# Layer-0 attention: scaling the heads' outputs instead of their probabilities

## The chip, the cores and the metric

One program runs on one core of a Trainium2 chip. The metric is the device time of one execution, in microseconds. The kernel before was run three times (1480.88, 1485.19 and 1488.71 us), and one further execution was profiled.

## The reference, cut to what matters

A sequence of 512 tokens of width 1024 goes through three layers. Layer 0 mixes windowed attention (8 query heads of 64 columns, 2 key/value heads) with a pooling branch, layer 1 mixes dense latent attention with a recurrent block, and each is followed by an MLP. A third block holds sparse attention, dilated attention and a gate. The change concerns layer 0's attention alone. Each query block of 128 sees the keys of its own and the two neighbouring blocks, and a learned sink enters the denominator:

```python
m = jnp.maximum(jnp.max(s, axis=-1, keepdims=True), sk)
p = jnp.exp(s - m)
p = p / (jnp.sum(p, axis=-1, keepdims=True) + jnp.exp(sk - m))
out = jnp.einsum('bnhgqj,bnjhd->bnqhgd', p.astype(v.dtype), vb)
```

Here the division is by row of `p`, one number for each query and head, so it can also be made on `out`.

## The kernel before, in words

Activations lie transposed: 128 channels on the partitions, 512 tokens along the free axis. A product in float32 is made of three TensorE passes over operands split in two parts (`hi`, `lo`), so every weight unit and every activation has a split: the `hi` part by `copy` (line 581, ScalarE or GpSimd, whichever the program takes to be free first), the `lo` part by `tt` (line 591, VectorE or GpSimd) or by VectorE.

The order of the instructions on each engine is fixed when the program is written out. A planner keeps a clock of its own (`fl.now`), which each matmul moves on, and a guess of when VectorE, ScalarE and GpSimd come free, made of a cost for each operation (`cost`, line 329). Work that evacuates or splits is a task: a generator that goes on when its due time has come on the planner's clock (`chains`, line 387). The engines themselves take their instructions in the written order and wait by semaphores. So a task that is written early on a wrong guess makes the engine wait on the chip, with all that is queued behind it.

Layer 0's attention runs under `fl.run(attend(...), fill, fl.share)`. `attend` (line 1141) writes the scores of up to three heads ahead of their products, and lets the products of three heads go on side by side. Where attention can't go on, the program takes a step of `fill`: the query blocks, then the pooling branch, then the first half of the output projection (`out_proj`, line 1197), which uses only the pooling branch. The second half, which uses the heads' outputs `yhl[4]` to `yhl[7]`, is appended when attention is written out, and then the rest of `fill` is run.

A head goes so. `score` writes three score tiles, each followed by a task `expo`: VectorE takes the row maximum (`mx`) and its negative (`nm`), ScalarE the exponential (`p`) with its row sum (`den`). When the three tasks are done, `finish` (line 1049) adds the sink's term (`es`), takes the reciprocal (`w4`; the trace writes it as `w`), and `weigh` (line 1066) multiplies the four query blocks of `p` by it, each with one `copy` (`p<-p,w` in the trace). Only then does `weigh` set `self.done`, for which `apply` (line 1094) waits. `apply` transposes `p` on TensorE (`tr<-cst,p`, line 565), splits the transposes from PSUM into `ph` and `pl`, and multiplies by `v` (`av`). `combine` (line 1132) adds the two halves of the result into `ya`: ScalarE copies one half (`cmb`), VectorE adds the other. Two heads share one `ya`; after the second one `store` (line 1373) splits it into `yhl[4 + i]` (`hi<-ya`, `lo<-ya`).

PSUM's eight banks are shared by four tags; `tr`, the tag of the transposes, may hold five of them in this phase.

Of the kernel before, what the change touches and what calls it, by code (L numbers as in the profile page):

```python
# [13 lines left out]
AF = mybir.ActivationFunctionType  # L14
# [4 lines left out]
P = 128  # L19
# [3 lines left out]
NQ = T // P  # L23
# [465 lines left out]
def tile_hybrid(ctx: ExitStack, tc: tile.TileContext, wt, xT, pT, prm_d, cst_d, out):  # L489
# [6 lines left out]
    V, S, G = (_Engine(fl, e, k) for e, k in ((nc.vector, "V"), (nc.scalar, "S"), (nc.gpsimd, "G")))  # L496
# [13 lines left out]
    def uid(s):  # L510
        cnt[0] += 1
        return f"{s}{cnt[0]}"

    def blk(name="b", dt=F32, n=T):
        return bp.tile([P, TB], dt, tag="b", bufs=NB, name=uid(name))[:, 0:n]

    def small(n, name="s", dt=F32):
        return sp.tile([P, n], dt, tag=f"s{n}", bufs=24, name=uid(name))
# [6 lines left out]
    def bank(tag):  # L525
        spare = len(banks) - sum(1 for k in held if k != tag and not held[k])
        if held[tag] >= getattr(fl, tag) or spare < 1 or min(banks) > fl.now:
            return None
        banks.remove(min(banks))
        held[tag] += 1  # L530
        return pp.tile([P, T], F32, tag="ps", bufs=8, name=uid(tag))
# [6 lines left out]
    def takec(tag):  # L538
        while (t := bank(tag)) is None:
            yield 0.1  # L540
        return t

    def give(tag):
        banks.append(max(fl.now, fl.last) + 0.1)
        held[tag] -= 1
# [6 lines left out]
    def waitc(*tasks):  # L552
        for t in tasks:
            while not t.done:
                yield 0.1
# [8 lines left out]
    def tr(o, i, idn):  # L564
        PE.transpose(o, i, idn)  # L565
        fl.now += 0.11
# [37 lines left out]
    class Unit:  # L604
        def __init__(self, name, i, cuts=1):
            self.name, self.i = name, i
            t = _WT[name]
            self.n = min(1024, _WN[t][1] - 1024 * i)
            self.left = self.n
            self.raw = self.hi = self.lo = self.task = None  # L610
            self.parts = [(self.n * c // cuts, self.n * (c + 1) // cuts) for c in range(cuts)]
            self.at, self.ready = [], 0
            self.kept = None
# [162 lines left out]
    def C(name, n=None):  # L776
        o = _CO[name][0]
        n = n or _CO[name][1]
        if o + n <= NKEEP:
            return cst[:, o:o + n]  # L780
        t = blk("cst")
        nc.sync.dma_start(t[:, :n], cst_d[:, o:o + n])
        return t

    def PR(name, i=0, n=1):
        o, w = _PO[name]
        return prm[:, o + i:o + i + n]

    ident = C("ident")
# [42 lines left out]
    def split_to(act, ps, scale=None):  # L832
        act.hi, act.lo = blk("hi", F32R), blk("lo", F32R)
        yield from split_ps(ps, act.hi, act.lo, scale)
        yield
        act.done = True
# [155 lines left out]
    class Head:  # L992
# [2 lines left out]

        def __init__(self, passes, rng, masks, v, scale=1.0, nsink=None, sink=None, gate=None):
            self.passes, self.rng, self.masks, self.v = passes, rng, masks, v
            self.scale, self.nsink, self.sink, self.gate = scale, nsink, sink, gate  # L1000
            self.done = False
            self.join = None

        def expo(self, qbs, ps):
# [44 lines left out]
        def finish(self, tasks):  # L1049

            yield from waitc(*tasks)
            if self.sink is not None:
                es = small(4, "es")
                S.activation(es, self.nm, AF.Exp, bias=self.sink, scale=1.0)
                yield
                V.tensor_add(self.den, self.den, es)
            else:
                V.tensor_scalar(self.den, self.den, 1e-30, None, op0=ALU.max)
            w4 = small(4, "w4")
            V.reciprocal(w4, self.den)  # L1060
            if self.gate is not None:
                V.tensor_mul(w4, w4, self.gate)
            yield
            yield from self.weigh(w4)

        def weigh(self, w4):
            for qb in range(NQ):
# [64 lines left out]
    def combine(po, dst):  # L1132

        t = blk("cmb")
        copy(t[0:64], po[64:128])
        yield
        V.tensor_add(dst, po[0:64], t[0:64])
        give("av")
        yield
# [21 lines left out]
    SC64 = 0.125  # L1161
# [53 lines left out]
    def next_norm(gcol, *sums):  # L1215

        h = acts()

        def then(c):
            go(split_to(h[c], x[c], gcol(c)))  # L1220
            for ss, sc in sums:
                go(ss.add(x[c], None if sc is None else sc(c)))
            yield

        return h, then
# [3 lines left out]
    h = acts()  # L1229
# [26 lines left out]
    nsink = cons.tile([P, 8], F32, name="nsink")  # L1256
# [113 lines left out]
    fill = [q_blocks(), pooling(), out_proj("eout", yhl, 0)]  # L1370
    yz = {}

    def store(hd, base, post=None):

        def done(po):
            i = hd // 2
            if i not in yz:
                yz[i] = [blk("ya"), 0]
            y = yz[i][0]
            yield from combine(po, y[64 * (hd % 2):64 * (hd % 2) + 64])  # L1380
            yz[i][1] += 1
            if yz[i][1] == 2:
                del yz[i]
                if post is not None:
                    yield from post(i, y)
                yield from split_to(yhl[base + i], y)
        return done

    def job0(hd):
        st = {}  # L1390

        def score():
            g = hd // 4
            q = qs[hd]
            st["h"] = Head([(q, ks[g][0]), (q, ks[g][1])], band3, band3_masks, lambda kb: v0[0](kb, g),
                           SC64, nsink=nsink[:, hd:hd + 1], sink=PR("sink", hd))
            return st["h"].score()

        return (lambda: hd in qs and 1 in ks and v0 and nmask.done, score,
                lambda: st["h"].apply(done=store(hd, 4)))  # L1400

    fl.phase("a")
    fl.run(kv_blocks(), None)
    fl.run(attend([job0(i) for i in range(8)], fl.ahead, fl.streams), fill, fl.share)
    ss = SumSq(NC)
    h, then = next_norm(lambda c: PR("n_mlp0", c), (ss, None))
# [98 lines left out]
    h = h2  # L1505
# [255 lines left out]
    def job1(hd):  # L1761
        st = {}

        def score():
            (qh, ql), (kh, kl) = qt[hd], kt[hd]
            st["h"] = Head([(qh, kh), (ql, kh), (qh, kl)], full, {},
                           lambda kb: vt[hd // 2](kb, hd % 2))
            return st["h"].score()

        return (lambda: hd in qt and hd in kt and hd // 2 in vt, score,  # L1770
                lambda: st["h"].apply(done=store(hd, 4)))
# [10 lines left out]
    h, then = next_norm(lambda c: PR("n_mlp1", c), (ss, None))  # L1782
# [15 lines left out]
    h = h2  # L1798
# [326 lines left out]
    def nsa_jobs(hd):  # L2125
# [41 lines left out]
        def app():  # L2167
            yield from st[0].apply(last=False, before=cmp_apply)
            yield from st[1].apply(first=False, prev=st[0], done=store(hd, 2, gate_z))
# [217 lines left out]
    h = h2  # L2387
# [26 lines left out]
```

## Time and profile before

| | |
|---|---|
| three runs | 1480.88, 1485.19 (median), 1488.71 us |
| profiled execution, its own time | 1481.19 us |
| its span, first to last instruction | 1479.4 us |
| mean granted TensorE clock | 0.993 |
| TensorE busy | 1450.2 us (98%) |
| VectorE busy | 906.4 us (61%) |
| ScalarE busy | 639.5 us (43%) |
| GpSimd busy | 328.3 us (22%) |
| DMA | 291.44 MB, mean 197 GB/s |

Busy times are sums over the whole span; the share in one stage can be very different. PE is TensorE, PEld its weight loads, DVE is VectorE, ACT is ScalarE, POOL is GpSimd. Most instructions are written by a helper, so they share a line (L561 matmuls, L565 transposes, L363 all of the three other engines) and are told apart by the names of their tiles.

### The profile page before, as it was taken

Reading aid. Unit: us, or ns where it says so; the run is one execution under the profiler, and the core shown is the slowest. Engines: PE = TensorE matmul, PEld = TensorE weight load, DVE = VectorE, ACT = ScalarE, POOL = GpSimd, SP = SyncE. Lnnn points to the kernel's source line nnn. Section 1 sums busy time; section 2 is a strip of 40 time slices with the busy share of each in tenths; the row PEclk is TensorE's granted clock in tenths of the full one; section 3 lists DMA queues with packets and bytes.
Section 4 is the critical chain, followed back from the end, with each engine's and each line's share of the span. In section 5 each row is a group of like instructions: output and inputs, shape, how many; then the busy total and the mean of one; then the engine's idle time right before and its main releaser. Section 6 shows DMA issues by size and latency. Waiting matters only on the chain.

```text
span 1479.4 us, 18899 instructions
## 1 busy us (share of the span) xinstructions
PE 1450.2 (98%) x6789; PEld 1175.9 (79%) x6789; DVE 906.4 (61%) x1414; ACT 639.5 (43%) x1175; POOL 328.3 (22%) x307
## 2 busy tenths in 40 slices
PE   8999999999999999799999999999999999999998
PEld 5777878888888887688888888888887788888787
DVE  7896865646434458987675665756755566536413
ACT  5684433323223345477343433334521575324623
POOL 5441220202102026542120210202110000110332
PEclk9999999999999999899999999999999999999999
DMA  6113688898333363331599999999855323346352
GB/s 220 44 43 100 209 276 284 284 290 283 108 100 101 141 221 130 127 129 72 188 312 332 334 325 331 320 334 320 305 204 201 114 86 115 114 174 216 109 196 88
DMA packets 118317, 291.44 MB, mean 197 GB/s; under 512 B 13136, under 2 KB 14672, under 8 KB 118224
## 3 DMA queue, kind: packets, MB, share of 16 engines
q1 hardware_dynamic: 118080, 289.98, 57.7%
q8 instruction: 53, 0.87, 0.2%
q14 instruction: 40, 0.33, 0.1%
q10 hardware_dynamic: 144, 0.26, 0.1%
HBM read 205.26 MB, written 84.93 MB: 196 GB/s over the span
## 4 chain that ended last, share of the span: by engine, by line
PE 90%; DVE 5%; DMA 2%; ACT 1%; issue 1%; POOL 0%; SPq 0%; POOLq 0%; DVEq 0%; ACTq 0%
PE mm L561 78%; PE sc L561 4%; PE tr L565 3%; PE av L561 3%; DVE sg L363 2%; PE tr L561 1%; DMA kr<-in_wt_dram 1%; DVE lo L363 1%; DVE wl L363 1%; DMA pin<-in_pT_dram 0%; DMA x<-in_xT_dram 0%; ACT wh L363 0%; DMA wk<-khi 0%; ACT sg L363 0%; POOL ma L363 0%
## 5 line engine op out<-in xcount | busy, mean ns | idle before, releaser
L561 PE MATMUL mm<-hi,wh 128*128 128x512 f32 (+1 forms) x1276 | 508.4, 398 | 0.8 <-POOL wh L363 0.5
L561 PE MATMUL mm<-hi,wl 128*128 128x512 f32 (+1 forms) x1276 | 502.1, 393 | 4.8 <-DVE wl L363 2.7
L561 PE MATMUL mm<-lo,wh 128*128 128x512 f32 (+1 forms) x1276 | 500.2, 392 | 0.3 <-POOL lo L363 0.3
L561 PEld LDWEIGHTS mm<-hi,wl 128*128 128x128 f32 x1276 | 241.0, 189 | 56.1 <-DVE wl L363 4.2
L561 PEld LDWEIGHTS mm<-lo,wh 128*128 128x128 f32 x1276 | 240.9, 189 | 55.3 <-POOL lo L363 0.8
L561 PEld LDWEIGHTS mm<-hi,wh 128*128 128x128 f32 x1276 | 241.2, 189 | 53.0 <-issue 1.1
L363 ACT ACTIVATE khi<-kr 128x512 fp32r<-128x512 f32 x120 | 75.9, 632 | 304.6 <-DMA kr<-in_wt_dram 298.3
L561 PE MATMUL mm<-ul,wh 128*128 128x512 f32 x512 | 201.6, 394 | 0.3 <-DVE ul L363 0.3
L561 PE MATMUL mm<-uh,wh 128*128 128x512 f32 x512 | 201.6, 394 | 0.0
L561 PE MATMUL mm<-uh,wl 128*128 128x512 f32 x512 | 201.5, 394 | 0.0
L363 DVE TENSOR_TENSOR wl<-wr,wh 128x1024 fp32r<-128x1024 f32 (+1 forms) x145 | 182.9, 1262 | 6.2 <-ACT wh L363 5.6
L363 DVE TENSOR_TENSOR klo<-kr,khi 128x512 fp32r<-128x512 f32 x150 | 121.4, 810 | 81.8 <-ACT khi L363 73.1
L363 ACT ACTIVATE wh<-wr 128x1024 fp32r<-128x1024 f32 (+1 forms) x147 | 148.8, 1013 | 47.6 <-PE mm L561 34.4
L363 DVE TENSOR_TENSOR x<-x,mm 128x512 f32<-128x512 f32 x112 | 76.8, 686 | 147.1 <-PE mm L561 143.7
L363 POOL TENSOR_TENSOR ma<-ma 128x512 f32<-128x512 f32 x62 | 86.6, 1397 | 279.3 <-ACT uh L363 237.6
L561 PEld LDWEIGHTS mm<-ul,wh 128*128 128x128 f32 x512 | 96.1, 188 | 23.8 <-DVE ul L363 1.3
L561 PEld LDWEIGHTS mm<-uh,wl 128*128 128x128 f32 x512 | 96.2, 188 | 22.3
L561 PEld LDWEIGHTS mm<-uh,wh 128*128 128x128 f32 x512 | 96.1, 188 | 22.3
L363 ACT ACTIVATE p<-sc,nm 128x512 f32<-128x512 f32 (+3 forms) x136 | 75.3, 557 | 27.8 <-DVE nm L363 24.8
L363 POOL TENSOR_SCALAR khi<-kr 128x512 fp32r<-128x512 f32 x30 | 29.6, 986 | 248.1 <-DMA kr<-in_wt_dram 225.8
L363 DVE TENSOR_TENSOR pl<-tr,ph 128x512 fp32r<-128x512 f32 (+2 forms) x108 | 66.3, 624 | 27.9 <-ACT ph L363 27.1
L363 DVE SCALAR_TENSOR_TENSOR ma<-mm,rb 128x512 f32<-128x512 f32 x64 | 44.1, 690 | 59.0 <-PE mm L561 58.9
(293 smaller groups left out, 1633.4 us busy)
## 6 DMA issues: line engine op xcount, KB each, us to landing
wr<-in_wt_dram SPq DMA_DIRECT2D x144, 512.0 KB, 5.2
kr<-in_wt_dram SPq DMA_DIRECT2D x150, 256.0 KB, 5.8
wk<-khi SPq DMA_DIRECT2D x150, 256.0 KB, 5.9
wk<-klo SPq DMA_DIRECT2D x150, 256.0 KB, 5.7
wh<-wk SPq DMA_DIRECT2D x74, 512.0 KB, 3.3
wl<-wk SPq DMA_DIRECT2D x74, 512.0 KB, 4.2
x<-xs SPq DMA_DIRECT2D x16, 256.0 KB, 5.0
cst<-in_cst_dram SPq DMA_DIRECT2D x8, 256.0 KB, 5.1
```

The costliest lines, as they stand in the source:

```text
L363: return fn(*a, **k)
L561: PE.matmul(o, l, r, start=start, stop=stop, skip_group_check=True)
L565: PE.transpose(o, i, idn)
```

## The change: what it does

For layer 0's heads `finish` writes the reciprocals into a column range of a tile `w8` that two heads share (8 columns: 4 query blocks of 2 heads), and `weigh` isn't called. `self.done` is set as soon as the exponentials are done, ahead of the sink's term and the reciprocal. The probabilities stay unscaled through the transposes and the product with `v`. When both heads of a pair stand in `ya`, `weigh_pair` spreads the 8 columns into a block `wb` of 128x512 on ScalarE (64 columns for each query block and head), transposes it in four pieces of 128x128 on TensorE into a `tr` bank, and multiplies `ya` by that bank on VectorE. Then `ya` is split as before. The heads of the other layers keep `weigh`.

```diff
-        def __init__(self, passes, rng, masks, v, scale=1.0, nsink=None, sink=None, gate=None):
+        def __init__(self, passes, rng, masks, v, scale=1.0, nsink=None, sink=None, gate=None, w4=None):
...
-            self.done = False
+            self.w4 = w4
+            self.done = self.weighed = False
...
             yield from waitc(*tasks)
+            self.done = self.w4 is not None
...
-            w4 = small(4, "w4")
+            w4 = small(4, "w4") if self.w4 is None else self.w4
             V.reciprocal(w4, self.den)
...
             yield
-            yield from self.weigh(w4)
+            self.weighed = True
+            if self.w4 is None:
+                yield from self.weigh(w4)
...
+    def weigh_pair(heads, w8):
+
+        def post(i, y):
+            while not all(h.weighed for h in heads):
+                yield 0.1
+            t = blk("wb")
+            S.activation(t.rearrange("p (b h e) -> p b h e", b=NQ, h=2),
+                         w8.rearrange("p (h b) -> p b h", h=2).unsqueeze(3).to_broadcast([P, NQ, 2, 64]), AF.Copy)
+            yield
+            ps = yield from takec("tr")
+            for b in range(NQ):
+                tr(ps[:, b * P:(b + 1) * P], t[:, b * P:(b + 1) * P], ident)
+            yield
+            V.tensor_mul(y, y, ps)
+            give("tr")
+            yield
+        return post
...
+    pairs = [([], small(8, "w8")) for _ in range(4)]
+
     def job0(hd):
         st = {}
+        heads, w8 = pairs[hd // 2]
...
-                           SC64, nsink=nsink[:, hd:hd + 1], sink=PR("sink", hd))
+                           SC64, nsink=nsink[:, hd:hd + 1], sink=PR("sink", hd),
+                           w4=w8[:, 4 * (hd % 2):4 * (hd % 2) + 4])
+            heads.append(st["h"])
...
-                lambda: st["h"].apply(done=store(hd, 4)))
+                lambda: st["h"].apply(done=store(hd, 4, weigh_pair(heads, w8))))
```

## Rows read from the trace of the kernel before

**Rows 1.** The page, its head and busy times: engine, busy us, share, instructions.
```profile
span 1479.4 us, 18899 instructions
PE 1450.2 (98%) x6789; PEld 1175.9 (79%) x6789; DVE 906.4 (61%) x1414; ACT 639.5 (43%) x1175; POOL 328.3 (22%) x307
```
**Rows 2.** Busy time by stretch around attention: stretch, its length, busy us, clock, DMA.
```profile
46.00:84.00 38.00, 37.97 (x205) 30.87 (x204) 33.52 (x79) 29.02 (x76) 14.86 (x21) 1.00 0.13 43
84.00:113.00 29.00, 24.57 (x142) 19.50 (x141) 26.58 (x60) 25.78 (x63) 15.40 (x15) 1.00 0.17 49
113.00:124.00 11.00, 11.00 (x60) 9.37 (x59) 7.22 (x13) 5.66 (x11) 1.78 (x2) 1.00 0.32 112
124.00:164.00 40.00, 40.00 (x177) 32.45 (x175) 28.67 (x41) 18.09 (x28) 3.23 (x2) 1.00 0.37 118
```
**Rows 3.** What TensorE waited for, 40 to 125 us: total us, times, longest.
```profile
PE av L561 <- DVE pl L363: 2.3, 2, 1.9
PE mm L561 <- DVE wl L363: 1.2, 2, 0.6
PE av L561 <- ACT ph L363: 0.4, 1, 0.4
PE mm L561 <- POOL lo L363: 0.3, 1, 0.3
```
**Rows 4.** Groups by shape, 40 to 125 us: count | busy us, mean ns.
```profile
L363 ACT ACTIVATE p<-p,w 128x384 f32<-128x384 f32 x13 | 7.8, 608 | 0.0
L363 ACT ACTIVATE p<-p,w 128x256 f32<-128x256 f32 x10 | 5.0, 503 | 2.1 <-DVE w L363 2.1
L363 POOL TENSOR_SCALAR p<-p,w 128x256 f32<-128x256 f32 x6 | 2.9, 484 | 10.0 <-DVE w L363 5.8 <-PE mm L561 3.6 <-ACT ph L363 0.6
L363 POOL TENSOR_SCALAR p<-p,w 128x384 f32<-128x384 f32 x3 | 1.8, 590 | 1.3 <-ACT p L363 1.3
L363 DVE TENSOR_TENSOR rbb<-tr,cst 128x512 f32<-128x512 f32 x3 | 2.1, 685 | 0.0
L363 ACT ACTIVATE zs<-mm 128x512 f32<-128x512 f32 x2 | 1.1, 574 | 0.0
```
**Rows 5.** The chain of waits, 120 to 170 us: start, us, what.
```profile
168.12 0.44 PE tr L565 x4
```
**Rows 6.** ScalarE in order of time: head 0's copies; ahead of two weight splits.
```profile
52.24 0.56 ACT L363 ACTIVATE p<-sc,nm 128x384 f32<-128x384 f32 x1
57.20 1.02 ACT L363 ACTIVATE p<-p,w 128x256 f32<-128x256 f32 x2 [1.40 <-DVE w L363]
60.41 0.50 ACT L363 ACTIVATE p<-p,w 128x256 f32<-128x256 f32 x1
...
83.85 0.60 ACT L363 ACTIVATE p<-p,w 128x384 f32<-128x384 f32 x1
84.36 1.05 ACT L363 ACTIVATE wh<-wr 128x1024 fp32r<-128x1024 f32 x1
...
95.65 0.61 ACT L363 ACTIVATE p<-p,w 128x384 f32<-128x384 f32 x1
96.16 1.05 ACT L363 ACTIVATE wh<-wr 128x1024 fp32r<-128x1024 f32 x1
```
**Rows 7.** All engines in order of time around the longest wait.
```profile
108.17 2.37 POOL L363 TENSOR_TENSOR wl<-wr,wh 128x1024 fp32r<-128x1024 f32 x1
109.37 2.25 DVE L363 TENSOR_TENSOR wl<-wr,wh 128x1024 fp32r<-128x1024 f32 x1 [0.58 <-ACT wh L363]
111.54 0.55 DVE L363 TENSOR_TENSOR pl<-tr,ph 128x384 fp32r<-128x384 f32 x1
112.14 0.45 PE L561 MATMUL av<-pl,v 128*128 128x384 f32 x1 [1.94 <-DVE pl L363]
```
**Rows 8.** The end of attention, VectorE and GpSimd in order of time.
```profile
125.60 2.17 POOL L363 TENSOR_TENSOR lo<-ya,hi 128x512 fp32r<-128x512 f32 x1 [9.02 <-ACT hi L363]
...
125.41 1.22 DVE L363 TENSOR_TENSOR wl<-wr,wh 128x1024 fp32r<-128x1024 f32 x1
135.95 0.69 DVE L363 TENSOR_TENSOR x<-x,mm 128x512 f32<-128x512 f32 x1 [2.10 <-PE mm L561]
```
**Rows 9.** What TensorE waited for, whole span: the longest.
```profile
PE tr L565 <- DVE vz L363: 8.0, 1, 8.0
PE mm L561 <- DVE wl L363: 2.7, 3, 1.4
```

## The prediction

> **What bounds the kernel now.** I read the busy times first: TensorE is busy for 1450.2 us of a span of 1479.4 [rows 1]. A change to VectorE, ScalarE or GpSimd can therefore give back 29.2 us at most in the whole program, and only where TensorE now stands still because of them. The share of one engine over the span says little for one stage, so the second view was the busy time by stretch around layer 0's attention [rows 2]. From 46 to 84 us TensorE works for 37.97 of 38.00 us: nothing can be gained there by relieving others. From 84 to 113 us it works for 24.57 of 29.00 us, so 4.43 us are idle, while VectorE is busy for 26.58 and ScalarE for 25.78 of 29.00. From 113 to 164 us TensorE is never idle. So the change has one pocket to gain from, of 4.43 us. The third view, TensorE's waits from 40 to 125 us, says whom it waits for there: the low half of a probability tile (2.3 us in two waits, one of them 1.9), the low half of a weight unit (1.2 us in two), the high half of a probability tile (0.4) and the low half of another operand, named "lo" there (0.3) [rows 3]. They sum to 4.2 of the 4.43 us.
>
> **What is removed.** All 32 scaling copies of the eight heads: 13 and 10 on ScalarE, 7.8 + 5.0 = 12.8 us, and 6 and 3 on GpSimd, 2.9 + 1.8 = 4.7 us [rows 4]. They are a load on two queues and also a delay in each head: head 0's last exponential ends at 52.24 + 0.56 = 52.80 us, its last scaling copy at 60.41 + 0.50 = 60.91 us [rows 6], and the transposes wait for it. Now they may follow the exponential, some 8 us earlier for this head, because the sink's term and the reciprocal no longer stand ahead of them either. That time is not a gain by itself: TensorE is full between 46 and 84 us with other work of the same stage, which has to be done anyway. It moves heads forward and leaves more fill for later.
>
> **What is added, for each of four pairs.**
> - TensorE: four transposes of 128x128. Four such float32 transposes in a row take 0.44 us on the chain [rows 5], so 4 x 0.44 = 1.76 us. TensorE is what the stage is bound by, so I count this in full.
> - ScalarE: one spread of 8 columns into 128x512. No row before has such a source. Below stands the copy of 128x512, 0.574 us; above, the scaling copies carried on to 512 columns: (608 - 503) / 128 x 128 + 608 = 713 ns [rows 4]. I take 0.6 us, near the row of the same output shape, so 2.4 us in all. Against 12.8 us removed, ScalarE loses 10.4 us of work in the stage.
> - VectorE: one product of `ya` with a PSUM bank. The rotary product that reads a PSUM bank and a 128x512 tile takes 0.685 us [rows 4], so 4 x 0.685 = 2.74 us in all, on an engine that is already the busiest beside TensorE.
>
> The remaining edits (the shared `w8`, the two flags) add no instruction; the reciprocal is written to another address. No DMA and no issue on a queue of SP or GpSimd is added or moved by hand.
>
> **What lies beside other work.** The new steps follow one another: spread, transposes, product, then the split. At 0.6 + 0.5 + 0.69 us and the hand-overs that is about 2 us more before a pair reaches `yhl`. The pairs are read by the second half of the output projection alone. At the end the last pair's low part ends at 125.60 + 2.17 = 127.77 us, and the eighth product of the first half is taken up by VectorE at 135.95 us [rows 8]; the second half can't start sooner. So 8.2 us of cover stand against 2 us, and this step costs nothing. Without that cover it would cost its 2 us once.
>
> **What comes back on TensorE.** Of the 4.43 us of waiting, the two weight waits (1.2 us) come after weight splits that ScalarE began late: at 84.36 us right behind a scaling copy that began at 83.85, and at 96.16 us behind another that began at 95.65 [rows 6]. Without these copies each split begins about 0.5 to 1 us earlier, as much as was waited, so I count both waits as gone. The longest wait, 1.94 us, is behind a VectorE weight product of 2.25 us, which had itself waited 0.58 us for ScalarE [rows 7]. The same form takes 1.22 us at 125.41 us [rows 8]. It was stretched while GpSimd ran its own weight product (108.17 to 110.54 us) [rows 7]. With ScalarE freer that product may start sooner and the other one may not be given to GpSimd; half of this wait, 1.0 us, is my estimate. Against this, VectorE gets 2 x 0.685 = 1.37 us for the two pairs that end in this stretch: 26.58 + 1.37 = 27.95 us of 29.00 [rows 2]. As long as its work is what it is, the stretch can't fall below about 27.95 us, a gain of 1.05; with the stretched product back at 1.22 us it could reach 26.92, a gain of 2.08. All of the waits would be 4.43. I take 2.2 us, half of the pocket, and keep 1.05 and 4.43 as ends.
>
> The Trainium skill, page "SBUF — State Buffer", section "Who interferes with whom", says that a VectorE instruction with two SBUF inputs contends with a GpSimd instruction that reads SBUF, and that whichever issued first holds the shared ports to its end. The two products above overlap as that rule has it, 2.25 against 1.22 us; by the rule alone 1.03 us of the longest wait would go only if GpSimd's product goes too, which no edit asks for.
>
> The same skill, page "TensorE: Matmul & The Clock Gate", section "Back-to-back issue gap", gives 134 cycles at 2.4 GHz for 128 columns, 0.056 us; by that the 16 transposes would be 0.9 us (an estimate from the page). The trace has 0.11 us each for float32 transposes, and that is used.
>
> **The sum.** 1.76 - 2.2 = -0.44 us. The profiled execution took 1481.19 us for a span of 1479.4, so it would take 1480.75. The median of the three runs is 1485.19, 4.0 us above that execution, and the runs spread from 1480.88 to 1488.71. I put the change against the median: 1484.8 us. A change of less than 0.5%, 7.4 us, can't be told from none here, and this one is far below it.
>
> **Rivals.**
> - All waits of the pocket go: 1.76 - 4.43 = -2.67 us, 1482.5 us. For it: every wait is at the end of a chain through ScalarE or VectorE. Against it: VectorE's 27.95 us.
> - Slower, by transposes written too early. TensorE takes its instructions in the written order. If the planner writes the four transposes when it believes `wb` is done, and ScalarE is behind, TensorE waits with all matmuls of the fill behind it. The longest wait that such a lag now causes is 1.94 us [rows 7]; four of that size give 4 x 1.94 + 1.76 = 9.5 us, 1494.7 us. It passes 0.5% from (7.4 - 1.76) / 4 = 1.4 us for each pair. Against it: ScalarE gets emptier, and 80 transposes of probabilities, which also wait for ScalarE, show no wait of their own in [rows 3].
> - The written order after the stage changes. The planner goes on with other guesses, and its choices of engine shift. The largest wait of the program, 8.0 us in layer 1, is of this kind: a transpose written ahead of a VectorE product that came late [rows 9]. Gone, it would give 1485.2 - 0.4 - 8.0 = 1476.8 us; another one of its size would give 1492.8. Against both: between the two attentions lies an MLP of some 450 us, over which the planner should fall into the same step again.
> - The earlier start isn't used: the heads are held by other things (the query blocks, three heads ahead), the waits stay, and only 1.76 us are added, 1487.0 us.
>
> **How the numbers follow.** Forecast 0.62; all waits gone 0.10; early transposes 0.09; the order after it better 0.10, worse 0.05; start not used 0.04. Faster by over 0.5%: 0.10, from the order after it, and 0.02 from the run spread, 0.12. Slower by over 0.5%: 0.09 + 0.05 = 0.14. Within 0.5%: 0.74. The range: the forecast's own cases run from 1482.5 to 1487.0 us; three runs of before spread by 4.3 us below and 3.5 above their median, which gives about 1479 to 1490, and taking in half of the outer cases 1477.5 to 1492.
>
> **What the profile after would show.** No `p<-p,w` before 130 us; four `wb` of about 0.6 us, 16 more transposes, four VectorE products of about 0.69 us. ScalarE about 10 us less busy between 46 and 124 us, VectorE about 2.7 us more. Waits of TensorE in the pocket near 2.2 us. No wait of `hi<-ya` or of the second half of the projection on TensorE. The step on early transposes is wrong, and the rival right, if TensorE waits for `wb` in its list. The prediction is wrong if the layers after it show waits that differ by more than 5 us in sum, or if the pocket grows past 4.43 us.

## The result and the profile after

The change makes the kernel slower. Four runs of it have a median of 1498.37 us, four of the kernel before 1483.43 us; the ratio is 1.0095, with a 95% interval of 1.0077 to 1.0112. Compared again on another occasion it was 1.0105 [1.0090, 1.0120]. The forecast was 1484.8 us in a range of 1477.5 to 1492.0: no change, and the measured time is outside.

The head of the page and the first busy times of the kernel after, to be read against [rows 1]: the span is 17.8 us longer, TensorE is busy for only 7.7 us more of it.

```profile
span 1497.2 us, 18897 instructions
PE 1457.9 (97%) x6805; PEld 1181.0 (79%) x6805; DVE 917.2 (61%) x1420; ACT 628.3 (42%) x1154; POOL 321.9 (22%) x298
```

Where the time went is seen by dating one product in both traces: the last addition of the output projection to the residual stream (`x<-x,mm`), which ends layer 0's attention. It starts at 158.2 us before and at 175.0 after (the two lines, before and after):

```profile
158.21 0.69 DVE L363 TENSOR_TENSOR x<-x,mm 128x512 f32<-128x512 f32 x1 [0.83 <-PE mm L561]
175.03 0.69 DVE L363 TENSOR_TENSOR x<-x,mm 128x512 f32<-128x512 f32 x1 [0.83 <-PE mm L561]
```

Behind it both spans have about the same left, 1479.4 - 158.2 = 1321.2 and 1497.2 - 175.0 = 1322.2 us. So the layers after it take the same time to 1 us, and 16.8 us are lost in the first 175.

The busy times of the kernel after in the stretches of [rows 2] (stretch, its length, then PE, PEld, DVE, ACT, POOL busy, granted clock, DMA share, GB/s):

```profile
46.00:84.00 38.00, 35.36 (x194) 27.95 (x193) 33.76 (x73) 22.88 (x63) 10.07 (x13) 1.00 0.10 28
84.00:113.00 29.00, 26.90 (x150) 22.19 (x150) 26.39 (x60) 19.34 (x52) 10.56 (x12) 0.94 0.11 38
113.00:124.00 11.00, 6.86 (x40) 5.20 (x38) 8.68 (x14) 4.88 (x11) 6.71 (x6) 1.00 0.17 48
124.00:164.00 40.00, 35.81 (x140) 28.03 (x141) 22.45 (x29) 12.58 (x16) 2.46 (x1) 0.87 0.29 92
```

The pocket of 84 to 113 us did shrink, from 4.43 to 2.10 us of idle TensorE. Its waits there are now these two, against those of [rows 3], which all lay in it:

```profile
PE sc L561 <- DVE ya L363: 1.5, 1, 1.5
PE mm L561 <- DVE wl L363: 0.6, 1, 0.6
```

But the stretches that were full are not full any more: 2.64 us idle from 46 to 84, 4.14 from 113 to 124 and 4.19 from 124 to 164, where before there were 0.03, 0.00 and 0.00. In sum 13.07 us stand against 4.46, so 8.6 us more. And the granted clock, 1.00 in all these rows before, is below 1.00 in two of them.

TensorE's waits in the whole span of the kernel after, the longest of them (who waited for whom, total us, times, longest), against [rows 3, 9]:

```profile
PE tr L565 <- DVE vz L363: 7.9, 1, 7.9
PE mm L561 <- ACT hi L363: 6.7, 2, 6.0
PE mm L561 <- DVE wl L363: 3.7, 4, 1.9
...
PE tr L565 <- ACT wb L363: 0.2, 1, 0.2
```

The wait of 8 us in layer 1 is as it was. New is one of 6.0 us behind the high part of some tile, and the new spread `wb` is waited for only 0.2 us. All engines in order of time show what the tile is (start, us, engine, instruction, and in brackets the idle time before it):

```profile
115.37 0.68 DVE L363 TENSOR_TENSOR up<-mm,rb 128x512 f32<-128x512 f32 x1
116.23 1.07 POOL L363 TENSOR_TENSOR us<-up 128x527 f32<-128x527 f32 x1 [8.66 <-DVE up L363]
117.39 2.15 POOL L363 TENSOR_TENSOR lo<-ya,hi 128x512 fp32r<-128x512 f32 x1
119.49 1.07 POOL L363 TENSOR_TENSOR us<-us 128x525 f32<-128x525 f32 x1
120.59 0.70 DVE L363 TENSOR_TENSOR us<-us 128x521 f32<-128x521 f32 x1 [1.15 <-POOL us L363]
120.78 0.66 PE L565 MATMUL tr<-cst,wb 128*128 128x128 f32 x4
121.44 1.27 POOL L363 TENSOR_TENSOR us<-us 128x513 f32<-128x513 f32 x1 [0.88 <-PE tr L565]
122.74 1.51 DVE L363 SCALAR_TENSOR_TENSOR pd<-us,up 128x512 f32<-128x512 f32 x1 [0.73 <-POOL us L363]
123.80 2.65 POOL L363 TENSOR_TENSOR wl<-wr,wh 128x1024 fp32r<-128x1024 f32 x1
124.18 2.31 DVE L363 TENSOR_TENSOR ed<-us,cst 128x16 f32<-128x16 f32 x1
126.73 0.63 ACT L363 ACTIVATE hi<-pd 128x512 fp32r<-128x512 f32 x1 [6.00 <-DVE pd L363]
127.41 0.80 PE L561 MATMUL mm<-hi,wh 128*128 128x512 f32 x1 [5.97 <-ACT hi L363]
130.43 0.63 PE L561 MATMUL mm<-hi,wl 128*128 128x512 f32 x1
131.47 0.63 PE L561 MATMUL mm<-hi,wh 128*128 128x512 f32 x1
131.90 0.63 PE L561 MATMUL mm<-hi,wl 128*128 128x512 f32 x1
135.42 0.39 PE L561 MATMUL mm<-hi,wl 128*128 128x512 f32 x1
135.65 0.40 PE L561 MATMUL mm<-lo,wh 128*128 128x512 f32 x1
```

This is the fourth chain of the pooling branch, which belongs to the fill: four window sums, a difference, two small corrections, a split. It takes 12 us from 115.37 to 127.4. Some of that is queueing: GpSimd puts the split of a pair (`lo<-ya,hi`, 2.15 us) between the first two sums, and `ed` takes 2.31 us beside GpSimd's weight product. In the written order nothing is left for TensorE to do in the last 6 us: all products of all eight heads are already behind it. The product that waits is the pooling branch's own; the first block of the output projection, already begun, needs its result. Before, the same chain began at 95.47 us, in the midst of the heads, and when its product was due at 106.15 us TensorE hadn't been idle (no wait stands at that line):

```profile
95.47 0.68 DVE L363 TENSOR_TENSOR up<-mm,rb 128x512 f32<-128x512 f32 x1
106.15 0.39 PE L561 MATMUL mm<-hi,wh 128*128 128x512 f32 x1
```

After the wait the matmuls of 128x512 start 0.43 us apart instead of 0.23 (131.47 to 131.90 against 135.42 to 135.65), up to 135 us; the granted clock is 0.50 from 127 to 135 us, the lower of its two levels.

The sum of the loss, an estimate from these rows: 8.6 us more idle; the half-rate stretches, about 15 products at 127 to 135 us and some 8 at 84 to 87 us, each about 0.2 us longer, 4.6 us; 16 transposes at 0.11 us, 1.8 us. That is 15.0 of the 16.8 us. 0.75 us of the rest stood before attention began (the first score product starts at 43.06 us before and 43.81 after).

The new operations themselves cost what was forecast (groups of the kernel after, 40 to 135 us, as in [rows 4]):

```profile
L363 DVE TENSOR_TENSOR ya<-ya,tr 128x512 f32<-128x512 f32 x4 | 2.7, 679 | 0.0
L565 PE MATMUL tr<-cst,wb 128*128 128x128 f32 x16 | 2.6, 283 | 0.2 <-ACT wb L363 0.2
L363 ACT ACTIVATE wb<-w 128x512 f32<-128x512 f32 x4 | 2.5, 626 | 0.0
```

### The profile page after: what moved, and what is told of

It reads as the page before. It is cut to its first block, busy times and chain, and to the rows that moved or that the text cites. A ratio compares the mean times of both kernels' runs of the same rounds, so it can differ in the third digit from the quotient of the medians.

```text
span 1497.2 us, 18897 instructions
## 1 busy us (share of the span) xinstructions
PE 1457.9 (97%) x6805; PEld 1181.0 (79%) x6805; DVE 917.2 (61%) x1420; ACT 628.3 (42%) x1154; POOL 321.9 (22%) x298
## 4 chain that ended last, share of the span: by engine, by line
PE 71%; DVE 4%; DMA 3%; issue 1%; ACT 1%; POOL 1%; SPq 0%; POOLq 0%; DVEq 0%; ACTq 0%
PE mm L561 61%; PE sc L561 4%; PE tr L565 3%; PE av L561 3%; DMA kr<-in_wt_dram 2%; DVE sg L363 2%; PE tr L561 1%; DMA pin<-in_pT_dram 0%; DMA wk<-khi 0%; DMA wk<-klo 0%; DVE lo L363 0%; ACT wh L363 0%; POOL ma L363 0%; DVE wl L363 0%; DVE klo L363 0%
## 5 line engine op out<-in xcount | busy, mean ns | idle before, releaser
L363 DVE TENSOR_TENSOR wl<-wr,wh 128x1024 fp32r<-128x1024 f32 (+1 forms) x144 | 179.4, 1246 | 8.0 <-ACT wh L363 7.4
```

The source lines that it names most:

```text
L363: return fn(*a, **k)
```

## The experiments

Two theories. **O, the written order**: heads that count as done earlier are written earlier, less fill is written between them, and the last pooling chain is left with nothing beside it. **L, the load**: the spread, the transposes and the product overload VectorE or TensorE, or make TensorE wait.

The written order can be read from the program itself: how many of layer 0's 64 products with `v` (two for each of four key blocks of eight heads) stand on TensorE ahead of a given product. "Tail" is that number for the products of the fourth pooling tile: 46 before, 64 after, so there all heads are over. "Blocks" counts the projection blocks begun before the last `av`: 4 before, 1 after. (The expectations speak of five before; that count was one too high.)

| kernel | tail | blocks | ratio to before, 95% interval |
|---|---|---|---|
| before | 46 | 4 | 1 |
| the change | 64 | 1 | 1.0095 [1.0077, 1.0112] |
| e1 removal alone | 64 | 0 | 1.0094 [1.0066, 1.0121] |
| e13 early flag alone | 64 | 0 | 1.0090 [1.0073, 1.0106] |
| e2 additions alone | 46 | 3 | 1.0022 [1.0007, 1.0036] |
| e3 heads go on late | 48 | 4 | 1.0014 [1.0000, 1.0028] |
| e7 late, no post | 48 | 4 | 1.0024 [1.0013, 1.0035] |
| e8 two heads ahead | 44 | 4 | 1.0031 [1.0019, 1.0043] |
| e4 share 0.5 | 50 | 2 | 1.0035 [1.0021, 1.0050] |
| e10 share 1.0 | 40 | 6 | 1.0030 [1.0015, 1.0046] |
| e11 after the reciprocal | 52 | 2 | 1.0043 [1.0026, 1.0060] |
| e9 last pair waits | 48 | 2 | 1.0053 [1.0035, 1.0070] |

Every kernel with a tail of 64 loses 0.9% or more (e5, e6 and e12 below also have 64, and lose 1.00 to 1.08%); every one with 40 to 52 loses 0.14 to 0.53%. Two pairs differ by the order alone, with the same operations on both sides (the planner may give a few to another engine): the change against e3, and e1 against e7.

**e1, the removal alone.**

```diff
-                lambda: st["h"].apply(done=store(hd, 4, weigh_pair(heads, w8))))
+                lambda: st["h"].apply(done=store(hd, 4)))
```

> Removal alone: the probabilities stay unscaled, heads go on as soon as their exponentials are done, and nothing is multiplied at the end (no spread, no transposes, no product; the division by the sums is left out). Theory O (the written order: heads run ahead of the fill, and the last pooling chain is left with nothing beside it): still slow, 1493 to 1498 us, with a wait of TensorE of 4 to 7 us behind the high part of a pooling tile. Theory L (the added steps load VectorE and TensorE or wait there): 1479 to 1484 us, no such wait.

1499.03 us, 1 us above the expected range, with a wait of 6.4 us behind a pooling tile (TensorE's waits, 40 to 180 us, the longest):

```profile
PE mm L561 <- ACT hi L363: 7.2, 2, 6.4
```

Without any of the added steps the whole loss is there. L falls.

**e2, the additions alone** (the head's own scaling stays; `ones` is a tile of ones).

```diff
-                lambda: st["h"].apply(done=store(hd, 4)))
+                lambda: st["h"].apply(done=store(hd, 4, weigh_pair(ones))))
```

> Additions alone: the heads scale their probabilities as before, and each pair also goes through the spread, the four transposes and the product, with a tile of ones (the output is that of the kernel before). Theory O: the fill stands where it stood before, so 1483.4 plus 1.8 for the transposes and up to 3 for the load, 1484 to 1488 us. Theory L: most of the 15 us, 1494 us or more.

1489.04 us, 0.22%, 1 us above O's range and far from L's. That is some 3 us, of which the transposes would be 1.8 by the rows; what the added steps cost by themselves isn't resolved, since e7 below has none of them and is as slow.

**e13, the early flag alone**, one line in the kernel before:

```diff
             yield from waitc(*tasks)
+            self.done = self.sink is not None
             if self.sink is not None:
```

> One line added to the kernel before: a head counts as done as soon as its exponentials are done, and its copies are still made (they come after the transposes and are read by nobody, so the division by the sums is left out). No spread, no transposes of it, no product; ScalarE and GpSimd keep the copies. Theory O: as slow as the change or slower, 1496 to 1503 us, with a wait of over 4 us behind the last pooling tile. Theory L, or a gain from the copies that the change takes away and that hides part of its cost: 1490 us or less.

1496.92 us against 1483.17 of the kernel before, 0.90%. This kernel keeps all copies on ScalarE and GpSimd, adds nothing, and loses about as much as the change. Its waits of TensorE, 40 to 180 us:

```profile
PE mm L561 <- ACT hi L363: 5.9, 2, 5.1
PE tr L565 <- ACT p L363: 3.7, 4, 1.7
PE tr L565 <- POOL p L363: 1.4, 2, 1.1
```

The wait behind the pooling tile is there, 5.1 us. But the expectation is wrong that all copies come after the transposes: GpSimd writes `p` only in these copies, and TensorE's transposes wait for `p` 5.1 us in six waits, against 0.2 us in the change. So a part of this kernel's loss is its own, and e1, which has no copies, is the cleaner test of the early flag.

**e3, heads go on late**, with all of the change but the flag:

```diff
-            self.done = self.w4 is not None
...
             self.weighed = True
             if self.w4 is None:
                 yield from self.weigh(w4)
+            else:
+                for qb in range(NQ):
+                    yield 0.45
+                self.done = True
```

> The change, but a head goes on only after its reciprocal and four pauses of 0.45 us of the planner's clock, about when the four copies would have been written. Theory O: the order of before comes back, 1480 to 1486 us, no wait of over 3 us at the end of attention. Theory L: the added steps are all there, 1494 to 1499 us.

1487.47 us, 0.14%: 2.3 us above the kernel before, at 1485.16, and 1.5 us above O's range. The longest of its waits is 2.9 us. The pauses are a delay on the planner's clock alone, no instruction. TensorE is full again where the change had its wait (120 to 135 us):

```profile
120.00:127.00 7.00, 7.00 (x42) 6.12 (x41) 4.10 (x7) 2.46 (x5) 0.00 (x0) 1.00 0.24 75
127.00:135.00 8.00, 8.00 (x38) 6.50 (x37) 5.44 (x8) 4.32 (x6) 0.00 (x0) 1.00 0.23 68
```

**e11, a head goes on after its reciprocal**, without the pauses.

```diff
             self.weighed = True
+            self.done = self.w4 is not None
```

(and the early line taken out, as in e3)

> The change, with a head going on after its reciprocal and without pauses: between the change and the run with the four pauses. Two projection blocks are written among the heads (four with the pauses, one in the change). Theory O: between the two times, 1488 to 1494 us. Theory L: 1495 us or more.

1490.11 us, 0.43%: between the two, as O has it.

**e4 and e10, more fill beside attention; e8, scores two heads ahead.** One number each in the tuning line of layer 0.

```diff
-    "a": dict(slack=2, gc=0.3, gt=-0.6, gw=-0.5, low=1, lat=0.1, wide=1, mm=4, sc=2, tr=5, av=2, ahead=3,
-              streams=3, share=0.1),
+    ... share=0.5 (e4), share=1.0 (e10), ahead=2 (e8)
```

> The change, with the share of fill that is written beside attention raised from 0.1 to 0.5 in layer 0. Theory O: the pooling blocks are written earlier among the heads, 1481 to 1487 us, and the wait behind the last pooling tile is gone. Theory L: about as the change, 1495 to 1500 us, since all added steps are there.

> The change, with a share of fill of 1.0. Six blocks of the first half of the projection are written among the heads, more than the five of the kernel before. Theory O: 1482 to 1488 us, at or under the share of 0.5 (1489.6). Theory L: 1495 us or more.

> The change, with the scores written two heads ahead of the products and not three. Theory O: the written order is again close to that of before (five blocks of the first half of the projection among the heads, as there), 1482 to 1488 us. Theory L: 1495 us or more.

1489.60, 1489.92 and 1490.43 us; the expected ranges ended at 1487, 1488 and 1488, so O has the sign and the greater part, and is 2 to 3 us too low. Two different numbers, the share (at two values) and `ahead`, both put the fill back among the heads and give the same 0.3%. With the tail covered, six blocks among the heads are no better than two.

**e9, the last pair waits for the fourth pooling block**, the tail alone:

```diff
-        return (lambda: hd in qs and 1 in ks and v0 and nmask.done, score,
+        return (lambda: hd in qs and 1 in ks and v0 and nmask.done and (hd < 6 or len(pools) >= 4), score,
...
                 go(pool_chain(g, ps, wpl))
+                pools.append(g)
```

> The change, but the scores of heads 6 and 7 are not written before the fourth pooling block's products are. All else of the change is there. If what costs is the fourth pooling chain with nothing beside it (its twelve steps stand after the last products of the heads): the wait of 6 us behind the pooling tile goes, and 6 to 11 us of the 15 come back, 1487 to 1492 us. If the heads' early start costs in other places: 1495 us or more.

1493.40 us, 0.53%, above the expected 1487 to 1492. The wait of 6 us is gone (0.3 us behind a pooling tile), the granted clock is 1.00 from 46 to 180 us, and the last addition starts at 165.4 us instead of 175.0:

```profile
46.00:180.00 134.00, 125.19 (x636) 100.73 (x635) 107.85 (x212) 72.29 (x160) 31.25 (x31) 1.00 0.27 83
PE mm L561 <- DVE wl L363: 3.5, 2, 1.9
PE mm L561 <- DVE lo L363: 2.6, 2, 1.6
PE mm L561 <- ACT hi L363: 0.3, 1, 0.3
```

So covering the tail gives 9.6 us at the end of the stage, of the 16.8 (0.6 of them lie before attention, whose first score product starts at 43.17 us here and at 43.81 in the change). The other 7.2 us stay: TensorE is idle for 8.81 us in this stretch against 4.46 before, now in other waits for VectorE (the lines above), and the transposes take 1.8 us. The uncovered tail is thus the larger part of the loss and not all of it. Of the 9.6 us the whole time shows about half, since this execution has 1491.5 - 165.4 = 1326.1 us behind the stage, 3.9 more than the change had. Which part of that is the kernel's and which the execution's these runs don't tell: e5 and e12 below, which add products to the change inside the stage only, have 1324.8 and 1325.6.

**e7, late and without the post.**

```diff
-                lambda: st["h"].apply(done=store(hd, 4, weigh_pair(heads, w8))))
+                lambda: st["h"].apply(done=store(hd, 4)))
```

(on e3)

> Heads go on late as in the run that had the four pauses, and nothing is multiplied at the end (the division by the sums is left out): only the copies are gone, at about the order of before. Theory O: TensorE is the bound, so the freed ScalarE gives 0 to 2 us, 1483 to 1486 us, and the difference to the run with the pauses and the post is its 1.8 us of transposes. If the copies were what held the stage: 1480 us or less.

1488.43 us, 0.24%, a miss: it was to be 1.8 us below e3 and isn't, and it is above the expected range. The intervals of the two overlap, so the price of the post isn't resolved here. But at about the order of before, 32 copies less on ScalarE and GpSimd give no gain. Against e1, which does the same work in the early order, it is 0.7% faster.

**e6, no projection weights on GpSimd.**

```diff
-                tt(ALU.subtract, self.lo[:, c0:c1], r[:, c0:c1], f(self.hi[:, c0:c1]), fl.gw)
+                tt(ALU.subtract, self.lo[:, c0:c1], r[:, c0:c1], f(self.hi[:, c0:c1]), 9.0 if self.name[:4] == "eout" else fl.gw)
```

> The change as it is, with the low parts of the projection's weights never on GpSimd. In the change two VectorE steps of the last pooling chain took 1.51 and 2.31 us beside a GpSimd weight product of 2.65 us. If that overlap is what stretches them: they fall to about 0.7 and 0.2 us, VectorE gets 1.2 us for the weight product, the wait of 6 us falls to about 3 to 4.5 us and the time to 1494 to 1497 us. If they are slow for another reason: 1498 us.

In order of time, the same steps of the chain:

```profile
122.50 1.04 POOL L363 TENSOR_SCALAR wh<-wr 128x1024 fp32r<-128x1024 f32 x1
122.56 1.51 DVE L363 SCALAR_TENSOR_TENSOR pd<-us,up 128x512 f32<-128x512 f32 x1 [0.73 <-POOL us L363]
124.00 0.16 DVE L363 TENSOR_TENSOR ed<-us,cst 128x16 f32<-128x16 f32 x1
125.08 0.79 PE L561 MATMUL mm<-hi,wh 128*128 128x512 f32 x1 [3.82 <-ACT hi L363]
129.69 0.79 PE L561 MATMUL mm<-lo,wh 128*128 128x512 f32 x1 [0.95 <-DVE lo L363]
```

The small correction `ed` falls from 2.31 to 0.16 us and the wait from 5.97 to 3.82. The difference `pd` stays at 1.51 us, where 0.7 was expected; it runs beside GpSimd's high part `wh` of the weight, which this edit leaves in place (0.68 us in the kernel before). The time is 1499.30 us, 1.0100, where 1494 to 1497 was expected: nothing of it arrives. VectorE now does two weight products of 2.36 us together in front of the next tile, for which TensorE waits 0.95 us, and the last addition starts at 174.5 us, 0.5 earlier. The overlap lengthened the wait, but the tail is about as long without it.

**e5 and e12, TensorE kept busy in the wait.**

```diff
             ps2 = yield from take("mm")
+            if g == 3:
+                for _ in range(29):
+                    PE.matmul(ps2[:, 0:384], identb, mb[:, 128:512], start=True, stop=True, skip_group_check=True)
             yield from mm3g(ps2, wpl, g, 1, [a])
```

(e12: six of `PE.matmul(ps2, x[0][:, 0:P], x[1], ...)` instead)

> The change as it is, with 29 products of a mask (128x384) written just before the stalled product of the last pooling block, into the PSUM bank that it starts anew; the order of all else is unchanged. They fall into TensorE's wait of 6 us. If the half-rate stretch after that wait costs time of its own (theory: about 16 products at 0.43 instead of 0.23 us, so 3.2 us), the granted clock stays 1.00 from 127 to 135 us and the time falls by 2 to 4 us against the change, to about 1495. If the half rate costs nothing beside the wait: 1498 to 1499 us.

> The change, with six float32 products of 128x512 of the residual stream in the 6 us wait, in place of the 29 bf16 products of a mask, which left the half-rate stretch where it was. If work on full-width float data in the wait keeps the clock: granted clock 1.00 from 127 to 135 us, and 1494 to 1496 us. If not: the stretch stays and the time is 1498 to 1501 us.

1500.53 us (1.0106) and 1501.00 us (1.0108 [1.0092, 1.0125]). The products in the wait and the granted clock behind it, first e5, then e12:

```profile
121.51 4.88 PE L1367 MATMUL mm<-mb 128*128 128x384 bf16 x29
125.00:130.00 5.00, 2.72 (x13) 1.20 (x11) 4.61 (x6) 3.02 (x5) 1.69 (x1) 0.92 0.36 105
130.00:135.00 5.00, 5.00 (x11) 3.55 (x12) 1.74 (x3) 0.79 (x1) 0.00 (x0) 0.50 0.30 108
```

```profile
120.46 5.32 PE L1367 MATMUL mm<-x,x 128*128 128x512 f32 x12
125.00:130.00 5.00, 2.73 (x7) 0.78 (x5) 4.62 (x7) 3.82 (x5) 0.64 (x1) 1.00 0.38 105
130.00:135.00 5.00, 4.93 (x15) 3.91 (x16) 0.76 (x3) 0.01 (x1) 0.00 (x0) 0.66 0.30 105
```

In the change both of these stretches stand at 0.50. The bf16 products filled 4.88 us of the wait and the clock fell all the same, some 4 us later. With the float32 products the half-rate stretch is about half as long as with the bf16 ones. Neither made the kernel faster: both times are at or above the change's, and e5's is above either of the two expected. So the 4.6 us above are read from the spacing of the products; that the time comes back when the clock stays up is not shown, though e9, which has neither the wait nor the half rate, is the one that fits it.

**e14, the change again**, unchanged, beside e13.

> The change itself, on the chip of the run beside it: 1.0077 to 1.0112 of the kernel before, 1497 to 1502 us; it says with which time the kernels that were run later than the first comparison are to be compared.

1498.85 us against 1483.17, 1.0105 [1.0090, 1.0120]. The later kernels are read against both values.

## Why the prediction was wrong, step by step

- **The step that failed** is in "what is removed": "That time is not a gain by itself ... It moves heads forward and leaves more fill for later." The direction is right and the price is not. It was put at nothing because TensorE was full from 46 to 84 us with work "which has to be done anyway": the sum treated the fill as a pile of matmuls that may lie anywhere. But the fill is also a chain. The pooling block's chain over VectorE, GpSimd and ScalarE, 12 us long in the change, had been hidden by the heads; with the heads written first there was nothing left to hide its end, and TensorE stood for 5.97 us. The price of the earlier heads shows where the work is the same: the change costs 0.95%, and 0.14% with its heads held back (e3); without the added steps it is 0.94% (e1) and 0.24% (e7). Of the 16.8 us in the stage 9.6 come back when the tail alone is covered (e9); the rest is spread over smaller waits and the added transposes.
- **The cover was checked at the wrong end.** The prediction looked for what hides the last pair's longer way into `yhl` (8.2 us against 2 us, and no such wait showed) and not for what the heads themselves hide.
- **The rival "the written order after the stage changes"** was the nearest: right that the planner's order decides, wrong in the place. It looked behind an MLP of 450 us, where nothing moved (1321.2 against 1322.2 us), and not into the stage itself.
- **The rival of early transposes** is wrong in size: its sign came, a wait for `wb` in the list, but of 0.2 us and not 7.8. The rival that the earlier start isn't used is wrong too: it was used, and that was the loss.
- **The added terms held.** Spread 0.626 us (0.6), product 0.679 (0.685), 16 transposes. ScalarE lost 60.46 - 47.10 = 13.4 us from 46 to 124 us (10.4), VectorE gained 68.83 - 67.32 = 1.5 (2.7).
- **The gain in the pocket came out by luck.** It fell from 4.43 to 2.10 us, a gain of 2.33 (2.2). But the heads had moved, so other work lay there. The weight waits, both counted as gone, had not gone: from 40 to 125 us they are 2.7 us in three after, against 1.2 us in two before, and the longest, 1.9 us, lies just ahead of the pocket. And a wait of 1.5 us of a score product is new.
- **The sign to look for had been named**: the prediction is wrong "if the pocket grows past 4.43 us". It grew beside the pocket, in stretches that were full.
- **What stays open**: with the order put back, wholly or in part, 0.14 to 0.53% remain. e2 has the additions and e7 has none of them, and both are some 3 us slow; each has a slightly other order and a stretch below full clock (0.69 and 0.84 from 113 to 124 us, and 0.81 in e3). No run parts these. That the half-rate stretches cost 4.6 us is read from rows and not shown by a run.

## What to carry to other kernels

In a kernel whose order is written out ahead by a planner, taking a delay out of one chain is also a change of the schedule: before pricing it, list what was interleaved with that chain, and ask of each piece whether it is mere work or a chain with a latency of its own, and what will hide it when it comes last. An engine that is busy for 98% says how little relief of the others can give back; it doesn't say that its work will stay as tightly packed. And where a speed-up turns into a loss, put the old order back first (a pause of the planner costs no instruction): that splits order from work in one run.

## What the runs showed of the hardware

- A VectorE instruction of 128x16 took 2.31 us beside a GpSimd product of 128x1024 (2.65 us), and 0.16 us when that product was on VectorE instead (e6). The Trainium skill, page "SBUF — State Buffer", section "Who interferes with whom", says that a VectorE instruction with two SBUF inputs contends with a GpSimd instruction that reads SBUF, and that the shared port pair is an exclusive lock. The trace agrees: the small operation ends 0.04 us after the large one (124.18 + 2.31 = 126.49 against 123.80 + 2.65 = 126.45 us). In the same trace an addition of 128x4 (`den<-den,es`), 0.16 us in the median, took 1.27 us from 105.23 us on beside a GpSimd product that ran 1.62 us from 104.85 on: again 0.03 us between the two ends.
- TensorE's clock fell to its half level after a wait that had been filled with 4.88 us of bf16 products of a mask (e5), and for about half as long after one filled with 5.32 us of float32 products of data (e12); in both TensorE also stood idle for about 1 us before the next product. Whether the kind of product or these gaps decide isn't shown. In the kernel before, 4.43 us of idle time spread over 29 us left it at 1.00.
